# Six places of a decoder step re-ordered: casts, small operations and transposes

## The chip, the core and the metric

The kernel runs on one core of a Trainium2 chip. The core has five engines that run their own instruction streams in order: TensorE (PE in the profile; its weight loads are listed as PEld), VectorE (DVE), ScalarE (ACT), GpSimd (POOL) and SyncE (SP, which here only issues DMAs). They meet through semaphores. The metric is the device time of one execution in microseconds (us); lower is better. A line number such as L478 is a line of the kernel before.

## The reference, cut to what matters

One layer of a decoder: a normalisation with modulation, a large input projection, a gated short convolution beside a matrix memory with four heads (mLSTM), an output projection, a residual with layer norm, and then a feed-forward part with its own modulation, convolution, gate, down projection and layer norm. There are 256 prompt tokens and 8 x 4 sample tokens, 288 in all; the width is 2048, the feed-forward width 5632.

```python
mod = silu(c) @ w_ada + b_ada                   # six rows: shift, scale and gate, twice
u = layernorm(x) * (1 + sc1) + sh1
p = u @ w_in                                    # B, C, h, q, k, v, o and the gates
y = concat(conv_part(p), mlstm_part(p))
x = layernorm(ALPHA * x + (1 + g1) * (y @ w_out)) * ln1_g + ln1_b
u2 = layernorm(x) * (1 + sc2) + sh2
a, g = split(u2 @ w_up)
x = layernorm(ALPHA * x + (1 + g2) * ((silu(conv(a)) * g) @ w_down)) * ln2_g + ln2_b
```

All arithmetic is in float32.

## The kernel before, in words

**Layout.** Activations lie with 128 features on the partitions and the 288 tokens along the free dimension, so x, u, u2 and the like are 16 tiles ("chunks", index k) of 128 x 288. Weights stream from HBM: 309 items of 128 x 2048 (1 MB), each 16 blocks of 128 x 128, through a ring of seven `raw` buffers. The order of the items is laid down by `plan()`.

**A matmul in three passes.** Each weight half (8 blocks, 128 x 1024) is split into a rounded high part `whi` (ACT, L316) and a remainder `wlo` (DVE, L329), in rings of four buffers each. Activations are split in the same way (`uh`, `ul`; `u2h`, `u2l`; and so on). A block then costs three TensorE matmuls of 288 columns: high x low (L476), low x high (L477), high x high (L478). `next_block()` hands out the blocks. At the first block of a half it calls `split_to`, which splits the halves up to two ahead (`LOOK`; one ahead in the first 16 halves). At the fourth block (`PREHI`) it issues the next half's cast alone, so that ACT is ahead of DVE.

**Ticks.** Everything beside the weight stream is written as generators ("sides"). `next_block()` calls `tick()` once per block, before the block's three matmuls, and a side that has yielded n goes on n blocks later. The order in which a program line is emitted is the order in its engine's queue, so the numbers yielded decide what lies before what on every engine.

**The six places.**

1. *Sums of the first norm* (L1233 to L1248). In the output projection the 16 tiles `mix` are added to the residual (`residual`, L1107) and `stats(m)` gathers sums: squares on ACT (L1156, L1157), weighted sums on DVE (L1142, L1152). `barrier` (set at L1114) keeps `split_to` from going beyond the last weights of the projection. The cast at `PREHI` does not look at it. In the last tile, 11 blocks in, `late_sums` makes four TensorE sums (L1238); 12 blocks in, `up_split` lifts the barrier and splits one half of the up-projection.
2. *u2* (L1364 to L1385). Per chunk: `u2_t` (a 256-column product L1366 and two 32-column products for the sample tokens L1367, L1368, all DVE), a TensorE correction (L1373) into PSUM, its addition (L1377, DVE), the cast (L1379, ACT) and the remainder (L1385, DVE). Six tiles of the up-projection run chunk by chunk over it, 18 matmuls per chunk; one PSUM bank is left for the corrections.
3. *Restoring of x1* (`restore`, L1423). Three POOL operations per chunk (L1426 to L1428), one chunk each 12 blocks, the first 8 blocks after the side starts. It must be done when the first part's up-projection ends (`drain(back)`).
4. *Modulation's transposes* (`ada_finish`, L389). When a unit of the modulation is complete in PSUM, it is copied out (L398, DVE; the first by ACT, L400), transposed on TensorE (L406) `YA` = 5 blocks later, and added to its bias (L412, L416). Kind "h" are the five units for u, kind "f" the other four.
5. *Heads' turns* (L911 to L927). For each of four heads: two DVE operations `norm` (L897), 6 blocks later four TensorE transposes `hT` (L915) with four DVE operations that read them (L918, L919), 6 blocks later the next head. `drain(ml)` at the end of the first `o` tile forces what is left of it.
6. *u of group three*: the first projection runs over the chunks in groups (0-1, 2-3, 4-7, 8-11, 12-15), since a group's modulation arrives late. `make_u(k)` (L555) calls `modulate` (L487): one 256-column operation L488 and two 32-column ones L490 and L491, all DVE; then the cast L558 (ACT) and the remainder L563 (DVE). One chunk per block (`YU` = 1) while the tiles of the group before are still running. Those tiles rotate over three PSUM banks. Every other one is taken out by ACT (L965, with the addition on POOL, L966), the rest by DVE (L968).

Of the kernel before, what the change touches and what calls it, by code (L numbers as in the profile page):

```python
# [9 lines left out]
AF = mybir.ActivationFunctionType  # L10
ALU = mybir.AluOpType

P = 128
NP = 256
# [3 lines left out]
N = NP + NS  # L18
# [19 lines left out]
UP_AT = 12  # L38
SUMS2_AT = 10
ROWS_AT = 20  # L40
RES0 = 8
RES1 = 12
G2_EARLY = 6
MIX_LAST = 8
# [5 lines left out]
AT0 = 1.0  # L50
SMALL_AT = 8
YA = 5
YU = 1
U_POOL = ()
HP_POOL = 2
# [160 lines left out]
def body(tc, d, off, items, blocks):  # L216
    nc = tc.nc
    V, A, G, T = nc.vector, nc.scalar, nc.gpsimd, nc.tensor
    from contextlib import ExitStack
    ctx = ExitStack()  # L220
    with ctx:
# [12 lines left out]
        def nm(s):  # L234
            uid[0] += 1
            return f"{s}_{uid[0]}"

        def st(name, dt=F32):
            return slab.tile([P, N], dt, tag="t", name=nm(name))
# [7 lines left out]
        def smp(ap):  # L247
            return ap[:, NP:N].rearrange("p (b t) -> p b t", t=TS)

        def bc_t(ap):  # L250
            return ap.unsqueeze(2).to_broadcast([P, NB, TS])
# [3 lines left out]
        def sm(name):  # L255
            a, b = off[name]
            return small[:, a:b]
# [12 lines left out]
        raws, halves = {}, {}  # L270
# [3 lines left out]
        barrier = [len(items)]  # L274
        sides = []
        it_index = {}
        hlist = []
# [28 lines left out]
        def free():  # L306
            live[0] -= 1
            load()

        his = {}  # L310

        def split_hi(n):
            if n not in his:
                i, hf = hlist[n]
                his[n] = hip.tile([P, 1024], F32R, tag="w", name=nm("whi"))
                A.copy(his[n], raws[i][:, hf * 1024:(hf + 1) * 1024])  # L316
                return his[n]
            return his.pop(n)

        def split_to(n):  # L320

            while emitted[1] < min(n + 1, len(hlist)) and hlist[emitted[1]][0] < barrier[0]:
                i, hf = hlist[emitted[1]]
                if i not in raws:
                    return
                r = raws[i][:, hf * 1024:(hf + 1) * 1024]
                hi = split_hi(emitted[1])
                lo = lop.tile([P, 1024], F32R, tag="w", name=nm("wlo"))
                V.tensor_tensor(lo, r, hi.bitcast(F32), ALU.subtract)  # L329
                halves[emitted[1]] = (hi, lo)  # L330
                emitted[1] += 1
                if hf == 1:
                    raws.pop(i)
                    free()
# [28 lines left out]
        mod = pers.tile([P, 6, KB, 9], F32, name="mod")  # L363
# [25 lines left out]
        def ada_finish(unit):  # L389
            kind, first, nb = UNITS[unit]  # L390
            n = P * nb // 2 if kind == "h" else 512
            ps = ada_ps.pop(unit)
            t = []
            for i in range(0, n, 256):
                s = st("adat")
                w = min(256, n - i)
                if unit:
                    V.tensor_copy(s[:, 0:w], ps[:, i:i + w])  # L398
                else:
                    A.copy(s[:, 0:w], ps[:, i:i + w])  # L400
                t.append(s)
            yield YA
            nbs = n // P
            tp = mps("adatp")
            for b in range(nbs):
                T.transpose(tp[:, b * P:(b + 1) * P], t[b // 2][:, (b % 2) * P:(b % 2 + 1) * P], ident)  # L406
            for b in range(nbs):
                src = tp[:, b * P:(b + 1) * P].rearrange("p (s j) -> p s j", j=32)[:, :, 0:9]
                if kind == "h":
                    for ty in range(2):  # L410
                        sl = slice(first + b, first + b + nbs + 1, nbs)
                        V.tensor_tensor(mod[:, ty, sl, :], src[:, 2 * ty:2 * ty + 2, :],  # L412
                                        badd[:, ty, sl].unsqueeze(2).to_broadcast([P, 2, 9]), ALU.add)
                else:
                    sl = slice(b, 16, 4)
                    V.tensor_tensor(mod[:, first, sl, :], src,  # L416
                                    badd[:, first, sl].unsqueeze(2).to_broadcast([P, 4, 9]), ALU.add)
            if kind == "h":
                prev = None
                for k in range(first, first + nb):  # L420
                    if k == 1:
                        V.tensor_tensor(xh[1], xh[1], rstd0, ALU.mult)
                        make_ulo(*prev)
                        prev = None
                    uh = make_u(k)
                    if prev:
                        make_ulo(*prev)
                    prev = (k, uh)
                    yield YU
                make_ulo(*prev)  # L430
# [20 lines left out]
        def next_block():  # L451
            while items[pos[0]][0] != "w":
                take()
            i, b = pos
            n = first_half[i] + b // 8
            if b % 8 == 0:
                load()
                split_to(n + (LOOK if n >= EARLY else LOOK_EARLY))
            if b % 8 == PREHI and n >= EARLY:
                n3 = emitted[1]  # L460
                if n3 < len(hlist) and n3 not in his and hlist[n3][0] in raws:
                    split_hi(n3)
            hi, lo = halves[n]
            pos[1] += 1
            if b % 8 == 7:
                halves.pop(n)
            if b == 15:
                pos[0], pos[1] = i + 1, 0
            tick()
            b %= 8  # L470
            return hi[:, b * P:(b + 1) * P], lo[:, b * P:(b + 1) * P]
# [13 lines left out]
            return h, lo  # L485

        def modulate(dst, src, sc, sh, k, E=V):  # L487
            E.tensor_scalar(dst[:, 0:NP], src[:, 0:NP], mod[:, sc, k, 0:1], mod[:, sh, k, 0:1],  # L488
                            ALU.mult, ALU.add)
            E.tensor_tensor(smp(dst), smp(src), bc_t(mod[:, sc, k, 1:9]), ALU.mult)  # L490
            E.tensor_tensor(smp(dst), smp(dst), bc_t(mod[:, sh, k, 1:9]), ALU.add)  # L491

# [28 lines left out]
        for k in range(0, KB, 2):  # L521
            t = st("xsum")
# [366 lines left out]
        def mlstm_end():  # L889
            hS = normalise(S["num"], colS[:, 1:2], 8)  # L890
            yield 8
            V.tensor_scalar(mvt[:, :, 0], mv[:, :, 1], EPS, None, ALU.add)
            newton(mvt[:, :, 1], mvt[:, :, 0], mvt[:, :, 2])
            yield 8

            def norm(ht, i):
                V.tensor_scalar(ht[:, 0:256], ht[:, 0:256], mv[:, i, 0:1], mvt[:, i, 1:2],  # L897
                                ALU.subtract, ALU.mult)

            norm(hS, 8)  # L900
            yield 6
            pS = mps("hsT", 256)
            for et in range(2):
                T.transpose(pS[:, et * P:(et + 1) * P], hS[:, et * P:(et + 1) * P], ident)
            hsT = st("hsT")
            A.copy(hsT[:, 0:256], pS)
            mhn = sm("mhn")
            for h in range(H):
                for tt in range(2):
                    norm(hraw[h][tt], 2 * h + tt)  # L910
                yield 6  # L911
                for et in range(2):
                    ps = mps("hT", 256)
                    for tt in range(2):
                        T.transpose(ps[:, tt * P:(tt + 1) * P], hraw[h][tt][:, et * P:(et + 1) * P], ident)  # L915
                    i = 2 * h + et
                    o = st("hm")
                    V.tensor_scalar(o[:, 0:NP], ps, mhn[:, i:i + 1], None, ALU.mult)  # L918
                    V.tensor_scalar(o[:, NP:N], hsT[:, et * P + 32 * h:et * P + 32 * h + 32],  # L919
                                    mhn[:, i:i + 1], None, ALU.mult)  # L920
                    hm[i] = o
                yield 6
                hraw[h] = None
# [119 lines left out]
        for m in range(KB):  # L1043
            t = st("xa")
# [200 lines left out]
        def up_split():  # L1245
            yield UP_AT
            barrier[0] = len(items)
            split_to(upcoming_w())  # L1248

        def upcoming_w():  # L1250
            return emitted[1]
# [91 lines left out]
        R = st("R")  # L1343
# [12 lines left out]
        x1 = xa  # L1356
# [4 lines left out]
        fsv = fs[:, 0:KB * NB].rearrange("p (k b) -> p k b", b=NB)  # L1361
        V.tensor_tensor(fsv, mod[:, SC2, :, 1:9], g1v.unsqueeze(2).to_broadcast([P, KB, NB]), ALU.mult)

        def u2_t(k):  # L1364
            t = st("u2t")
            V.scalar_tensor_tensor(t[:, 0:NP], x1[k][:, 0:NP], gs[:, k:k + 1], R[:, 0:NP], ALU.mult, ALU.mult)  # L1366
            V.tensor_tensor(t[:, NP:N], x1[k][:, NP:N], R[:, NP:N], ALU.mult)  # L1367
            V.tensor_tensor(smp(t), smp(t), bc_t(fsv[:, k]), ALU.mult)  # L1368
            hold[k] = t

        def u2_corr(k):
# [41 lines left out]
        for j in (8, 12):  # L1413
            ps = mps("rb", N)
            tokens(ps, spread(j), P)
            t = st("rb")
# [6 lines left out]
        def restore():  # L1423
            yield RES0
            for k in range(KB):
# [414 lines left out]
```

## Time and profile before

| | |
|---|---|
| median of 3 runs | 1537.24 us (1536.14 to 1538.02) |
| the profiled execution | 1537.2 us |
| its span, first to last instruction | 1535.4 us |
| DVE busy | 946.3 us (62%) |
| ACT busy | 592.7 us (39%) |
| POOL busy | 226.4 us (15%) |
| DMA | 344.03 MB, mean 224 GB/s |
| mean granted TensorE clock | 0.997 |

The span is what the trace shows; 1.8 us of the execution's time lie around it. In a list of waits, "A <- B: t, n, m" says that A's engine sat idle before A for t us in n places, the longest m, until B released it. In a timeline a row has the start, the duration, engine, line, operation, the tiles written and read, the shape, a count, and in brackets the idle time before it and what ended it. In a table of windows each row has the stretch, its length, and for each engine the busy time and the number of instructions, then the granted TensorE clock as a share of full speed, the DMA share and GB/s.

### The profile page before, as it was taken

The page shows a single profiled execution, that of the slowest core. Times are in us where ns is not written, and L with a number is a line of the kernel's source. Part 1 is how long each engine was busy: PE and PEld are TensorE (multiplying, and loading weights), DVE is VectorE, ACT ScalarE, POOL GpSimd, SP SyncE. Part 2 cuts the span into 40 slices and gives each one's busy share as a digit, 9 for nine tenths or more (in the row PEclk, how much of TensorE's full clock was granted, in tenths as well). Part 3 has the DMA queues.
Part 4 walks back from the last instruction along what each step waited for, and adds up shares of the span by engine and source line. Part 5 has one row for each costly group of instructions (what it writes and reads, how often), then busy time and mean ns, then how long its engine had stood idle before and what let it go on. Part 6 is the DMA issues. An engine that isn't in the chain of part 4 may idle for free.

```text
span 1535.4 us, 28421 instructions
## 1 busy us (share of the span) xinstructions
PE 1516.2 (99%) x11849; PEld 1416.9 (92%) x11849; DVE 946.3 (62%) x1771; ACT 592.7 (39%) x891; POOL 226.4 (15%) x445
## 2 busy tenths in 40 slices
PE   9999999999999999999999999999999999999998
PEld 7988988888888889789999999999999999999997
DVE  6466567677775488697565545555555445555764
ACT  5542234422233434344334333444443334444442
POOL 3320005201025130005730000000000000000400
PEclk9999999999999999999999999999999999999999
DMA  9887778568899774474666544444445444444411
GB/s 392 340 343 287 304 292 338 222 254 298 330 375 357 291 276 170 163 274 183 228 221 229 190 163 169 161 165 165 165 172 181 154 166 167 166 168 166 156 58 62
DMA packets 50036, 344.03 MB, mean 224 GB/s; under 512 B 5950, under 2 KB 6254, under 8 KB 9454
## 3 DMA queue, kind: packets, MB, share of 16 engines
q1 hardware_dynamic: 47028, 329.21, 57.8%
q0 software_dynamic: 2736, 12.82, 2.1%
q8 instruction: 93, 1.52, 0.4%
q14 instruction: 35, 0.29, 0.1%
q10 hardware_dynamic: 144, 0.19, 0.0%
HBM read 329.88 MB, written 12.31 MB: 223 GB/s over the span
## 4 chain that ended last, share of the span: by engine, by line
PE 93%; DVE 4%; DMA 2%; ACT 1%; issue 1%; SPq 0%; DVEq 0%; ACTq 0%
PE dn L478 6%; PE dn L476 6%; PE dn L477 6%; PE g L476 6%; PE g L478 6%; PE g L477 6%; PE a L476 6%; PE a L478 5%; PE a L477 5%; PE adaps L383 5%; PE h L476 5%; PE h L477 4%; PE h L478 4%; PE mix L476 2%; PE mix L477 2%; PE mix L478 2%
## 5 line engine op out<-in xcount | busy, mean ns | idle before, releaser
L316 ACT CAST whi<-raw 128x1024 fp32r<-128x1024 f32 x410 | 424.0, 1046 | 373.9 <-PE dn L478 125.8
L329 DVE TENSOR_TENSOR wlo<-raw,whi 128x1024 fp32r<-128x1024 f32 x410 | 502.6, 1242 | 52.2 <-ACT whi L316 51.5
L478 PE MATMUL dn<-y2h,whi 128*128 128x288 f32 x704 | 207.9, 295 | 0.0
L476 PE MATMUL dn<-y2l,whi 128*128 128x288 f32 x704 | 207.7, 295 | 0.0
L477 PE MATMUL dn<-y2h,wlo 128*128 128x288 f32 x704 | 207.4, 295 | 0.0
L477 PE MATMUL a<-u2h,wlo 128*128 128x288 f32 x656 | 193.6, 295 | 0.8 <-DVE wlo L329 0.8
L478 PE MATMUL g<-u2h,whi 128*128 128x288 f32 x656 | 193.9, 296 | 0.0
L478 PE MATMUL a<-u2h,whi 128*128 128x288 f32 x656 | 193.8, 295 | 0.0
L476 PE MATMUL a<-u2l,whi 128*128 128x288 f32 x656 | 193.6, 295 | 0.0
L477 PE MATMUL g<-u2h,wlo 128*128 128x288 f32 x656 | 193.4, 295 | 0.0
L476 PE MATMUL g<-u2l,whi 128*128 128x288 f32 x656 | 193.3, 295 | 0.0
L476 PE MATMUL h<-ul,whi 128*128 128x288 f32 x512 | 156.4, 305 | 2.4 <-DVE hp L968 1.5
L477 PE MATMUL h<-uh,wlo 128*128 128x288 f32 x512 | 152.2, 297 | 0.0
L478 PE MATMUL h<-uh,whi 128*128 128x288 f32 x512 | 151.9, 297 | 0.0
L477 PEld LDWEIGHTS dn<-y2h,wlo 128*128 128x128 f32 x704 | 132.3, 188 | 0.1
L476 PEld LDWEIGHTS dn<-y2l,whi 128*128 128x128 f32 x704 | 132.3, 188 | 0.1
L478 PEld LDWEIGHTS dn<-y2h,whi 128*128 128x128 f32 x704 | 132.2, 188 | 0.0
L476 PEld LDWEIGHTS a<-u2l,whi 128*128 128x128 f32 x656 | 123.2, 188 | 5.0 <-issue 4.2
L476 PEld LDWEIGHTS g<-u2l,whi 128*128 128x128 f32 x656 | 123.2, 188 | 3.4 <-ACT hal L1545 2.5
L477 PEld LDWEIGHTS a<-u2h,wlo 128*128 128x128 f32 x656 | 123.0, 188 | 1.1 <-DVE wlo L329 1.1
L478 PEld LDWEIGHTS g<-u2h,whi 128*128 128x128 f32 x656 | 123.4, 188 | 0.0
L478 PEld LDWEIGHTS a<-u2h,whi 128*128 128x128 f32 x656 | 123.3, 188 | 0.0
(475 smaller groups left out, 2788.0 us busy)
## 6 DMA issues: line engine op xcount, KB each, us to landing
raw<-wst SPq DMA_DIRECT2D x300, 1024.0 KB, 4.8
raw<-cst SPq DMA_DIRECT2D x8, 1024.0 KB, 4.9
cs_o<-raw POOLq DMA_DIRECT2D x8, 1024.0 KB, 10.4
xa<-xT POOLq DMA_DIRECT2D x16, 144.0 KB, 9.9
y_o<-yo SPq DMA_DIRECT2D x9, 256.0 KB, 2.5
xin<-xT SPq DMA_DIRECT2D x5, 432.0 KB, 5.6
cp_o<-cnew POOLq DMA_DIRECT2D x8, 128.5 KB, 7.2
raw<-wst SPq DMA_DIRECT2D x2, 512.0 KB, 13.7
```

The source lines that it names most:

```text
L316: A.copy(his[n], raws[i][:, hf * 1024:(hf + 1) * 1024])
L329: V.tensor_tensor(lo, r, hi.bitcast(F32), ALU.subtract)
L383: T.matmul(ps[32 * s:32 * s + 32, 0:n], csil[:, k, :], r[:, c0:c0 + n], start=(k == 0), stop=(k == 15))
L476: T.matmul(ps, hi, ul, start=start, stop=False)
L477: T.matmul(ps, lo, uh, start=False, stop=False)
L478: T.matmul(ps, hi, uh, start=False, stop=stop)
```

## The change

Six edits, all of order or of engine; no value that is computed changes.

```diff
-RES0 = 8
+RES0 = 70
...
+YF = 12
+U_ACT = (4, 5, 6, 7)
...
-            yield YA
+            yield YA if kind == "h" else YF
...
-                if n3 < len(hlist) and n3 not in his and hlist[n3][0] in raws:
+                if n3 < len(hlist) and n3 not in his and hlist[n3][0] in raws and hlist[n3][0] < barrier[0]:
                     split_hi(n3)
...
         def modulate(dst, src, sc, sh, k, E=V):
-            E.tensor_scalar(dst[:, 0:NP], src[:, 0:NP], mod[:, sc, k, 0:1], mod[:, sh, k, 0:1],
-                            ALU.mult, ALU.add)
+            if k in U_ACT:
+                A.activation(dst[:, 0:NP], src[:, 0:NP], AF.Identity, scale=mod[:, sc, k, 0:1], bias=mod[:, sh, k, 0:1])
+            else:
+                E.tensor_scalar(dst[:, 0:NP], src[:, 0:NP], mod[:, sc, k, 0:1], mod[:, sh, k, 0:1],
+                                ALU.mult, ALU.add)
...
                 for tt in range(2):
                     norm(hraw[h][tt], 2 * h + tt)
-                yield 6
+                yield 9
...
         def up_split():
             yield UP_AT
             barrier[0] = len(items)
             split_to(upcoming_w())
+            yield 3
+            split_to(upcoming_w())
...
         def u2_t(k):
...
-            V.tensor_tensor(t[:, NP:N], x1[k][:, NP:N], R[:, NP:N], ALU.mult)
-            V.tensor_tensor(smp(t), smp(t), bc_t(fsv[:, k]), ALU.mult)
+            G.tensor_tensor(t[:, NP:N], x1[k][:, NP:N], R[:, NP:N], ALU.mult)
+            G.tensor_tensor(smp(t), smp(t), bc_t(fsv[:, k]), ALU.mult)
```

- Place 1: the cast at `PREHI` respects the barrier, and `up_split` splits a second half three blocks after the first.
- Place 2: the two 32-column products of u2 go from DVE to POOL.
- Place 3: the restoring starts 70 blocks after its side, not 8.
- Place 4: kind "f" units are transposed 12 blocks after they are copied out, not 5.
- Place 5: the heads' transposes follow their norm after 9 blocks, not 6.
- Place 6: for chunks 4 to 7 the 256-column operation of the modulation goes from DVE to ACT.

## The prediction

> **What bounds the kernel now.** I read the page first, then the list of waits with TensorE as the waiter, then windows and timelines at the six places.
>
> ```profile
> PE 1516.2 (99%) x11849; PEld 1416.9 (92%) x11849; DVE 946.3 (62%) x1771; ACT 592.7 (39%) x891; POOL 226.4 (15%) x445
> ...
> PE adatp L406 <- DVE adat L398: 1.7, 2, 1.0
> PE h L476 <- DVE hp L968: 1.5, 1, 1.5
> PE corr L1373 <- DVE u2t L1377: 1.2, 2, 1.0
> PE stat L1238 <- DVE ln1p L1152: 1.1, 1, 1.1
> ...
> PE a L477 <- DVE wlo L329: 0.8, 1, 0.8
> ...
> PE hT L915 <- DVE ht L897: 0.7, 1, 0.7
> ...
> PE h L476 <- ACT hpt L965: 0.4, 1, 0.4
> ```
>
> TensorE is busy 1516.2 of 1535.4 us. No edit touches a weight matmul, so only TensorE's idle time, 19 us, and the time in which its clock is low can be won. Seven rows of its waits belong to the six places: 1.7 + 1.5 + 1.2 + 1.1 + 0.8 + 0.7 + 0.4 = 7.4 us. The clock is in the windows; the first three are adjacent, 3.41 us each:
>
> ```profile
> 88.65:92.06 3.41, 1.83 (x12) 1.60 (x12) 2.61 (x8) 1.91 (x4) 0.81 (x1) 1.00 1.01 425
> 92.06:95.47 3.41, 3.41 (x16) 3.20 (x15) 3.41 (x5) 3.17 (x5) 3.07 (x4) 0.50 0.91 384
> 95.47:98.88 3.41, 3.41 (x27) 3.41 (x26) 2.97 (x5) 1.14 (x2) 0.00 (x0) 1.00 0.45 161
> 638.20:641.61 3.41, 2.29 (x12) 1.19 (x11) 2.02 (x3) 1.28 (x3) 0.00 (x0) 1.00 0.00 0
> ```
>
> After a stretch in which PE was busy for 1.83 of 3.41 us (54%), the granted clock was 0.50 for exactly the next 3.41 us: 16 matmuls instead of 27. Those 11 matmuls at 3.41 / 27 = 0.126 us are 1.4 us that no list of waits shows. The fourth row (67% busy) was not followed by a fall. So the limit lies somewhere between 54% and 67%.
>
> A wait also costs more than its row, because it breaks the pipeline. Here are the last matmul before the modulation's four transposes and the first after them, once with a wait and once without:
>
> ```profile
> 470.04 0.29 PE L478 MATMUL o<-uh,whi 128*128 128x288 f32 x1
> ...
> 471.49 0.38 PE L476 MATMUL o<-ul,whi 128*128 128x288 f32 x1
> ...
> 300.79 0.29 PE L478 MATMUL cg<-uh,whi 128*128 128x288 f32 x1
> ...
> 301.28 0.38 PE L476 MATMUL cg<-ul,whi 128*128 128x288 f32 x1
> ```
>
> From start to start it is 1.45 us against 0.49 us: 0.96 us lost where 0.6 us of idle time is listed. I add 0.3 us to each wait that goes, and 0.2 us where no transposes follow.
>
> **The change part by part.** *Place 4, modulation's transposes.* Two of the four late units wait, 0.6 and 1.0 us. The copies out sit behind other DVE work and end 0.3 us after TensorE would need them. Seven blocks more are 21 matmuls of 0.126 us, 2.6 us. That covers both waits, and the transposes still fall inside the same output tile. What moves along are four DVE additions per unit and one POOL DMA (the feed-forward state) that waits for the copy's buffer; it is needed 100 us later. The two units that do not wait move too and have no reason to begin. Gain: 1.7 + 2 x 0.3 = **2.3 us**.
>
> *Place 5, heads' turns.* The third head waits:
>
> ```profile
> 450.86 2.00 ACT L316 CAST whi<-raw 128x1024 fp32r<-128x1024 f32 x2 [7.44 <-DMA raw<-wst]
> ...
> 451.94 1.23 DVE L329 TENSOR_TENSOR wlo<-raw,whi 128x1024 fp32r<-128x1024 f32 x1 [0.36 <-ACT whi L316]
> 453.08 0.82 DVE L897 TENSOR_SCALAR ht<-ht,mv,mvt 128x256 f32<-128x256 f32 x2
> ...
> 469.16 0.46 DVE L1102 TENSOR_TENSOR sg<-sg,hm 128x288 f32<-128x288 f32 x1 [5.27 <-ACT sg L1101]
> ```
>
> A late weight DMA holds ACT, the remainder then holds DVE, and the norm is queued behind it. With 9 blocks the norm of this head itself comes 6 blocks later (two heads before it), behind the same remainder, and ends near 455. Its transposes come 15 blocks into their tile, near 457. The fourth head ends 12 blocks later than now, 14 blocks into the first `o` tile, two before `drain` would force it. Its DVE reads end near 468; the first `o` product that shares DVE is at 469.2. Sixteen transposes, eight norms and sixteen reads move, and no DMA. Gain: 0.7 + 0.3 = **1.0 us**.
>
> *Place 1, sums of the first norm.*
>
> ```profile
> 637.67 1.04 ACT L316 CAST whi<-raw 128x1024 fp32r<-128x1024 f32 x1 [7.88 <-DMA raw<-wst]
> ...
> 638.62 0.44 ACT L1156 ACTIVATE ln1q<-xa 128x288 f32<-128x288 f32 x1
> ...
> 640.03 0.65 PE L1238 MATMUL stat<-ln1p,pick 128*8 128x288 f32 x2 [1.12 <-DVE ln1p L1152]
> ```
>
> The early cast of the up-projection's first half holds ACT for 7.9 us until its weights land, and the squares of tile 14 are queued behind it. With the barrier respected, the squares run as soon as tile 14's residual is there, some 4 us sooner, and DVE's sums end well before TensorE is ready for the fourth one (640.03 - 1.12 = 638.9). The fourth sum then follows the third. The cast comes after the squares and still starts at 637.67, because the DMA sets it. Two casts and two remainders (1.04 and 1.22 us each) end near 641.2, before DVE's next duty, the residual of the last tile, which must wait for 0.65 us of sums and 18 matmuls, near 641.9. Cover: 0.7 us. If the weights land later than that, the excess is paid. The second half's split also frees its `raw` buffer, so SP issues one load some 18 us earlier. Gain: 1.1 + 0.2 = **1.3 us**.
>
> *Place 2, u2.* Two waits, 1.0 and 0.3 us:
>
> ```profile
> 658.20 2.36 DVE L329 TENSOR_TENSOR wlo<-raw,whi 128x1024 fp32r<-128x1024 f32 x2 [0.36 <-ACT whi L316]
> 660.48 0.45 DVE L1377 TENSOR_TENSOR u2t<-u2t,corr 128x288 f32<-128x288 f32 x1
> ...
> 660.98 0.40 PE L1373 MATMUL corr<-tok,cft 128*128 128x288 f32 x1 [0.97 <-DVE u2t L1377]
> ...
> 664.00:676.00 12.00, 11.98 (x90) 11.98 (x91) 11.43 (x32) 6.83 (x11) 0.00 (x0) 1.00 0.73 292
> ...
> L993 POOL COPY hal<-sffn x44: 188/281/1251, 591.4 to 1408.2; 128x16 f32<-128x16 f32 x44
> ...
> L602 POOL TENSOR_TENSOR cs<-xf x1: 215/215/215, 234.7 to 234.7; 4x24 f32<-4x24 f32 x1
> ```
>
> Two remainders stand before the addition L1377 that frees the correction's bank. One of them is the half that place 1 now splits in advance. The addition comes 1.2 us earlier, near 659.3, before TensorE is ready for the correction (660.98 - 0.97 = 660.0). The later wait hangs on the same chain (addition, cast, cast, remainder, addition), which moves 1.15 us while TensorE moves 1.2; I leave 0.1 to 0.2 us there. Gain: 1.2 + 2 x 0.2 - 0.3 = **1.3 us**, nearly all of it from the edit of place 1. The move to POOL itself I take at nothing. POOL sits idle here and DVE, busy 11.43 of 12.00 us, is not on TensorE's path (11.98 of 12.00). POOL's price is not in the trace: the nearest rows give 0.2 us for 24 columns and 1.25 us for the longest small copy beside DVE, so a pair costs 0.4 to 2.5 us per chunk. I take 0.5. A chunk lasts 2.5 us.
>
> *Place 3, restoring.*
>
> ```profile
> L999 DVE SCALAR_TENSOR_TENSOR ac<-hal,small,ac x44: 533/535/1122, 701.3 to 1421.2; 128x304 f32<-128x304 f32 x44
> ...
> 715.01 0.96 DVE L999 SCALAR_TENSOR_TENSOR ac<-hal,small,ac 128x304 f32<-128x304 f32 x1
> ...
> 716.89 1.21 DVE L329 TENSOR_TENSOR wlo<-raw,whi 128x1024 fp32r<-128x1024 f32 x1
> ```
>
> Beside POOL's products the convolution steps take 0.96 us instead of 0.535. Two of them stand directly before the remainder that TensorE awaits (0.8 us), and two pairs before those. Without POOL it comes at least 0.85 us sooner. The 48 operations start 62 blocks later, behind POOL's small copies of those tiles. They end at block 70 + 16 x 12 = 262 of the 384 that the part has left, and place 3 runs from there on as it now runs from 729, without a wait of TensorE. Gain: 0.8 + 0.2 = **1.0 us**.
>
> *Place 6, u of group three.*
>
> ```profile
> 86.07 0.42 DVE L412 TENSOR_TENSOR mod<-adatp,badd 128x18 f32<-128x18 f32 x4
> ...
> 88.25 0.40 ACT L965 ACTIVATE hpt<-h 128x288 f32<-128x288 f32 x1
> ...
> 90.59 0.43 ACT L558 CAST uh<-xc 128x288 fp32r<-128x288 f32 x1 [1.22 <-DVE xc L491]
> 90.78 0.45 DVE L968 SCALAR_TENSOR_TENSOR hp<-h,hp 128x288 f32<-128x288 f32 x1
> 90.92 1.04 ACT L316 CAST whi<-raw 128x1024 fp32r<-128x1024 f32 x1
> ...
> L781 ACT ACTIVATE d<-d,colP x4: 506/508/512, 304.3 to 385.9; 128x256 f32<-128x256 f32 x4
> ...
> 311.82 0.31 POOL L804 MEMSET vt<- 128x1 f32 x2 [2.91 <-PE kv L798]
> ...
> 313.10 0.37 ACT L803 COPY vt<-kv 128x256 f32<-128x256 f32 x1
> ```
>
> Four DVE operations become four on ACT; a 256-column one with an operand per partition takes 0.51 us there (L781). ACT then does 0.51 + 0.03 + 0.43 per chunk, and neighbours overlap by 0.1 (90.59 + 0.43 against 90.92), so 0.87 us. From 86.5 two chunks end at 88.26. The eviction hpt starts where it does now, and its 0.4 us wait stays. Chunk 6's cast ends near 89.55, its remainder at 90.05, and the eviction hp starts at 89.95 instead of 90.78: 0.8 us won. Behind it, ACT's next eviction (after the weight cast) ends at 91.65, where TensorE now wants it at 91.35: 0.3 us given back. Idle time in any 3.41 us is then at most about 1.2 us (65% busy), mostly under 1.0, so I take the fall of the clock as gone, 1.4 us. The last two rows carry the order: POOL's fill of one column of `vt`, emitted after the copy, ran before it, so disjoint columns of a tile do not wait for each other. Gain: 0.8 - 0.3 + 1.4 = **1.9 us**.
>
> The sum is 2.3 + 1.0 + 1.3 + 1.3 + 1.0 + 1.9 = 8.8 us. Made against the profiled execution, 1537.2 (span 1535.4 and 1.8 around it), which is also the median of the runs, it gives **1528.4 us**.
>
> **The rivals.** *The clock falls all the same.* Place 6 keeps some 1.1 us of waits; a window that catches most of them is 65% busy, close to the 54% that was followed by a fall. Time: 1528.4 + 1.4 = 1529.8. [...]
>
> *ACT and DVE take turns in place 6.* If the two column ranges of a chunk did wait for each other, a chunk would cost 0.51 + 0.4 + 0.43 us and more, as now. Nothing of the 1.9 is won: 1530.3. The `vt` rows speak against it.
>
> *POOL and DVE get in each other's way in u2.* DVE is 95% busy there; if POOL's pair lengthens DVE's steps by more than the 0.38 us it takes away, 13 chunks lose 0.1 to 0.3 us each: 1530 to 1532.5.
>
> *The waits come back a few blocks on* (norms and copies behind the next remainder, weights late at 641). Half of places 1, 4 and 5, and place 3, lost: 1532 to 1536.
>
> *Slower.* The mechanism is POOL's pair in u2. Above 2.5 us per pair, POOL sets the pace of the loop, and TensorE waits in each of 14 chunks. At 3.6 us (two of the 1.8 us that its longest 288-column product took) it costs 14 x 1.1 = 15.4 us: 1543.8. It decides from 3.3 us on (8.8 + 3.1 = 14 x 0.85). Against it: 32 columns, an idle engine, and 0.2 us for 24 columns.
>
> **How the numbers follow.** A measurement of this kernel can tell about 0.2% (3.1 us) from no change. Forecast, 1527 to 1529.4: 0.52. Clock: 0.16. Turns of ACT and DVE: 0.08. POOL against DVE: 0.10. Waits come back: 0.11, of which 0.07 within 0.2%. Slower: 0.03. The range 1526.8 to 1532.2 takes in the first four and what the added 0.2 to 0.3 us per wait may be off; it leaves out about 0.2. Faster 0.90, same 0.07, slower 0.03.
>
> **What would show it.** In the waits of TensorE, the rows of adatp on DVE, stat on ln1p, a on wlo and hT on ht are gone; corr on u2t keeps at most 0.3 us; hp keeps under 1 us; hpt keeps 0.4 and more. No window before the end has a clock under 1.00. ACT's cast after the projection starts with its DMA and after the squares. L999 is at 0.535 us until 728. POOL's two products per chunk take 0.2 to 0.6 us each. I am wrong if new rows of TensorE's waits add up to more than 1 us, or if the clock falls at another place.

## The result, and the profile after

The changed kernel took 1528.65 us (median of 6 runs, 1528.45 to 1529.39), the kernel before 1536.61 (6 runs, 1535.16 to 1538.02). The ratio is 0.9946, with a 95% interval of 0.9937 to 0.9956. So 8.0 us are gone in the medians; 8.8 were forecast, from 1537.2 to 1528.4 us. The profiled execution took 1528.45 us with a span of 1526.4.

Two rows of the changed kernel's page, the engines' busy time and the granted clock in 40 slices:

```profile
PE 1512.3 (99%) x11849; PEld 1414.9 (93%) x11849; DVE 944.6 (62%) x1735; ACT 594.5 (39%) x895; POOL 240.0 (16%) x477
...
PEclk9999999999999999999999999999999999999999
```

TensorE's busy time fell by 3.9 us though it runs the same 11849 products: the stretch at half the clock (3.41 us at 92.06 in the kernel before) and the refill behind each wait (0.17 to 0.5 us where it was read below) are counted there, and no list of waits shows them. The rest of the 9.0 us of span is idle time. The list of TensorE's waits in the changed kernel (engine and line, releaser: us in total, times, longest):

```profile
PE sq L542 <- ACT sq L540: 1.0, 1, 1.0
PE warm L524 <- POOL ones L369: 1.0, 1, 1.0
PE h L478 <- DVE hp L973: 0.8, 1, 0.8
PE h L478 <- ACT hpt L970: 0.8, 2, 0.6
PE rr L1343 <- DVE sv L1333: 0.7, 1, 0.7
...
PE corr L1380 <- DVE u2t L1384: 0.2, 1, 0.2
```

Of the seven rows of before, those of adatp on DVE, stat on ln1p, a on wlo and hT on ht are gone. corr on u2t went from 1.2 to 0.2, hp from 1.5 to 0.8, and hpt grew from 0.4 to 0.8 (0.55 and 0.23). This is the timeline of ACT and DVE at place 6, group three, in the changed kernel:

```profile
88.43 0.59 ACT L491 ACTIVATE xc<-xc,mod 128x256 f32<-128x256 f32 x1
...
89.05 0.43 ACT L563 CAST uh<-xc 128x288 fp32r<-128x288 f32 x1
...
89.39 0.60 ACT L491 ACTIVATE xc<-xc,mod 128x256 f32<-128x256 f32 x1
89.49 0.19 DVE L496 TENSOR_TENSOR xc<-xc,mod 128x32 f32<-128x32 f32 x1
...
89.97 0.45 DVE L973 SCALAR_TENSOR_TENSOR hp<-h,hp 128x288 f32<-128x288 f32 x1
...
91.30 0.70 ACT L970 ACTIVATE hpt<-h 128x288 f32<-128x288 f32 x2
```

ACT's 256 columns (89.39 to 89.99) and DVE's 32 of the same tile (89.49) run side by side, so the two ranges do not wait for each other. The eviction hp starts at 89.97, forecast 89.95. The next eviction hpt starts at 91.30 and holds TensorE for 0.23 us: this is the wait that was to be given back. The windows of the changed kernel there (us, length, busy PE, PEld, DVE, ACT, POOL with counts, granted clock, DMA share, GB/s):

```profile
86.67:90.09 3.42, 2.42 (x17) 1.96 (x15) 2.76 (x10) 3.29 (x9) 0.80 (x1) 1.00 1.01 405
90.09:93.50 3.41, 2.80 (x19) 2.57 (x20) 2.40 (x3) 3.41 (x6) 1.72 (x2) 1.00 1.02 430
93.50:96.91 3.41, 3.41 (x28) 3.41 (x27) 3.41 (x6) 2.18 (x3) 1.36 (x3) 1.00 0.55 185
```

71% and 82% busy, and the clock stays at 1.00.

### The profile page after: what moved, and what is told of

Same layout as the page of the kernel before. It is cut to its first block, busy times and chain, and to the rows that moved or that the text cites. A ratio compares the mean times of both kernels' runs of the same rounds, so it can differ in the third digit from the quotient of the medians.

```text
span 1526.4 us, 28419 instructions
## 1 busy us (share of the span) xinstructions
PE 1512.3 (99%) x11849; PEld 1414.9 (93%) x11849; DVE 944.6 (62%) x1735; ACT 594.5 (39%) x895; POOL 240.0 (16%) x477
## 3 DMA queue, kind: packets, MB, share of 16 engines
q8 instruction: 93, 1.52, 0.4%
## 4 chain that ended last, share of the span: by engine, by line
PE 96%; DVE 2%; ACT 1%; issue 0%; DMA 0%; SPq 0%; DVEq 0%; ACTq 0%
PE dn L480 6%; PE dn L479 6%; PE dn L478 6%; PE a L478 6%; PE a L480 6%; PE g L480 6%; PE g L478 6%; PE a L479 6%; PE g L479 6%; PE adaps L385 6%; PE h L478 5%; PE h L479 4%; PE h L480 4%; PE mix L478 2%; PE mix L479 2%; PE mix L480 2%
```

## The experiments

Twelve kernels ran, five rounds each. A median of five turned out too coarse for parts of 0.5 to 2 us, because two kinds of event land in some executions and not in others (a fall of the clock, 1.6 us; a late weight load, 1.3 us; both are shown below). So each part is read from the traces, by how much later than in the changed kernel the same product starts, counted in each trace from its own first `h` product (25.46 us in the changed kernel). The columns are the 445th `h` product (behind group three, 101.85), the first hsT (435.34), the first statc (640.09), the last corr (684.46) and the first yb (1509.00); the last column is where the profiled execution's clock fell before the end.

| kernel | h 445 | hsT | statc | last corr | yb | clock fell at |
|---|---|---|---|---|---|---|
| before | 1.68 | 1.70 | 6.05 | 7.07 | 8.71 | 92.06 |
| after_again | -0.02 | 0.28 | 0.25 | 0.27 | 0.26 | - |
| u6_group3 | 2.48 | 2.50 | 2.77 | 2.79 | 2.78 | 93.19 |
| u6_fill | 0.30 | 0.32 | 0.46 | 2.07 | 2.06 | 648.32 |
| yu2 | -0.13 | -0.26 | -0.22 | 1.40 | 1.93 | 647.61 |
| u4_turns | 0.01 | 0.03 | 2.29 | 2.29 | 2.14 | - |
| u5_heads | -0.08 | -0.06 | 0.39 | 0.46 | 0.80 | - |
| u1_cast | -0.03 | -0.02 | 1.43 | 1.44 | 0.75 | - |
| u1_second | 0.04 | 0.34 | 0.33 | 3.28 | 3.28 | 648.09 |
| u2_pool | -0.04 | -0.02 | 0.26 | 0.18 | 0.30 | - |
| u3_restore | -0.05 | -0.04 | 0.09 | 0.12 | 1.32 | - |
| tail_fill | 0.00 | 0.12 | 0.09 | 0.14 | 0.13 | - |
| best | 1.45 | 1.52 | 1.45 | 1.48 | 2.02 | - |

The second row is the changed kernel against itself: two of its executions differ by up to 0.3 us, so differences below that tell nothing. The yb column is less sure than the others: between the last corr and yb, u1_cast gains 0.7 us on the changed kernel and yu2 and best lose 0.5, in stretches where TensorE has no more waits than the changed kernel and where no edit of theirs acts. So a place is priced below close behind it, and not at yb.

Each execution also has a mean granted clock, traced or not. In every trace the clock is at half for the last 5.2 to 7.9 us (6.4 in the kernel before, 6.2 in the changed kernel), which takes 0.0017 to 0.0026 off the mean, and a fall before the end takes off another 0.0011. So, as an estimate from these traces, an execution with a mean of 0.998 had no fall, one with 0.997 at most one, and one with 0.995 at least two.

### Place 6 undone, and undone with its idle time filled

```
-U_ACT = (4, 5, 6, 7)
+U_ACT = ()
```

> The changed kernel with place 6 undone: chunks 4 to 7 are modulated on DVE again. Theory (two waits and the fall of the clock they bring): TensorE's waits on hpt and hp come back with 0.4 and 1.5 us, the 3.41 us after them run at clock 0.50, and the time rises by 1.9 us, to about 1530.5 us. [...]

The second kernel has the same edit and six products of the ones matrix with itself at the place of the long wait:

```
+FILL = 6
...
+                if g == 1 and t[1] == 22:
+                    fl = mps("fill", P)
+                    for _ in range(FILL):
+                        T.matmul(fl, ones, ones, start=True, stop=True)
```

> Place 6 undone as in u6_group3, and six further matmuls of 128 columns, whose result nothing reads, put on TensorE ahead of the tile that waits for hp (1.3 us of work inside a wait of 1.5 us). Theory (the clock falls when TensorE is busy for little more than half of a 3.41 us stretch): the tile starts when it did, the clock stays at 1.00, and the time is 1.4 us below that of u6_group3, about 1529.1 us. Rival (the fall comes from something else than idle time at this place): the clock falls all the same and the time is that of u6_group3, 1530.5 us.

Measured: 1530.22 us (ratio 0.9956, 0.9944 to 0.9969) and 1530.37 (0.9957, 0.9943 to 0.9970). The medians don't part them; the windows do. u6_group3:

```profile
89.78:93.19 3.41, 1.89 (x13) 1.44 (x12) 2.61 (x7) 2.08 (x5) 0.59 (x2) 1.00 1.01 425
93.19:96.60 3.41, 3.41 (x16) 3.41 (x15) 3.41 (x6) 2.99 (x4) 2.78 (x4) 0.50 0.82 344
```

u6_fill, at 90 and at 648 us:

```profile
88.54:91.95 3.41, 3.10 (x23) 2.92 (x24) 2.58 (x8) 1.91 (x5) 0.80 (x1) 1.00 1.02 430
91.95:95.36 3.41, 3.41 (x26) 3.20 (x25) 3.40 (x5) 3.30 (x5) 3.05 (x4) 1.00 0.72 296
644.91:648.32 3.41, 2.15 (x17) 1.61 (x13) 2.24 (x10) 1.19 (x4) 0.91 (x4) 1.00 1.01 411
648.32:651.73 3.41, 3.41 (x17) 0.59 (x16) 1.38 (x3) 1.37 (x2) 2.94 (x13) 0.50 1.02 430
```

Without place 6 the stretch at 90 us is 55% busy and the next runs at half the clock, with 16 products. With the hole filled it is 91% busy, the next keeps 1.00 with 26, and group three costs 0.30 us more than in the changed kernel, where the kernel before costs 1.68. So of place 6's 1.7 us, 0.3 are waits and 1.4 the clock. (u6_group3's 2.48 also has a wait of 0.45 us at 80 us that the kernel before does not have.) u6_fill lost 1.6 us later, between the start of rr (0.47) and the last corr (2.07): the last two rows show the clock at half there, at a place that no edit touched. No forecast had it for this kernel. Two of its untraced executions (1530.14 and 1530.76 us) have a mean clock of 0.998, so no fall, and what made them as long as the traced one is open.

### Group three's chunks two turns apart

```
-YU = 1
+YU = 2
```

> The changed kernel with YU = 2: one chunk of u per two blocks instead of per block, in all groups. Theory (what is left of place 6's waits, 0.55 + 0.83 + 0.23 us, is ACT and DVE doing four chunks within four blocks of TensorE): spread over eight blocks these waits go, with about 0.15 us of refill each, and the time falls by 1.5 to 2.0 us, to about 1526.9 us. Rival (the chunks then end too late for the group that needs them, here or in groups four and five): new waits of TensorE on ul or uh at the start of a group, time 1528.7 us or more.

Measured: 1530.44 us (0.9961, 0.9948 to 0.9973). The wait and the windows of yu2:

```profile
PE h L478 <- ACT hpt L970: 2.3, 1, 2.3
```

```profile
87.83:91.24 3.41, 1.53 (x12) 1.30 (x10) 1.99 (x6) 2.24 (x5) 0.35 (x1) 1.00 1.00 418
91.24:94.65 3.41, 2.98 (x22) 2.99 (x23) 2.57 (x7) 3.38 (x7) 2.19 (x4) 1.00 0.84 351
...
644.20:647.61 3.41, 2.15 (x21) 1.77 (x21) 2.04 (x11) 1.33 (x3) 1.10 (x4) 1.00 0.93 368
647.61:651.03 3.42, 3.42 (x17) 0.58 (x9) 1.30 (x3) 1.18 (x2) 3.03 (x12) 0.50 1.01 417
```

The three waits of group three became one, 2.3 us long against 1.6 in sum, and group three still ended no later (-0.13 us). Of that, 0.26 us had been won before 84 us, where a wait of 0.26 us near 54 us is gone; that the rest went with two waits' refills is likely and not shown. The 1.5 us that this was to win are not there. The stretch was 45% busy, less than in the kernel before, and no fall followed; a stretch at 644 us was 63% busy and a fall did follow. So the busy share by itself does not decide. The slowest execution of yu2 (1533.21 us, untraced) has a mean clock of 0.995, so at least two falls, and where they came is not known.

### Place 4 undone

```
-YF = 12
+YF = 5
```

> The changed kernel with place 4 alone undone: the modulation's transposes are given five turns again in place of twelve. Theory: TensorE's waits of 0.63 us near 470 us and 1.03 us near 587 us come back, and with the refill behind each the start of statc near 640 us is 2.3 us later than in the changed kernel's trace; 1530.9 us, or 1532.5 with a fall of the clock. Rival 1 (a wait costs its row and no more): 1.7 us later, 1530.3. Rival 2 (a wait removed there comes back at a later barrier, so place 4 was worth nothing): 0.0 to 0.5 us later, 1528.65 to 1529.1.

Measured: 1530.71 us (0.9959, 0.9946 to 0.9973). A row of u4_turns' list of waits, and a row of its timeline:

```profile
PE adatp L408 <- DVE adat L400: 1.7, 2, 1.1
```

```profile
642.59 0.38 PE L1297 MATMUL statc<-small,rows 8*128 8x8 f32 x2 [0.48 <-ACT rows L1294]
```

In the changed kernel the same product is at

```profile
640.09 0.83 PE L1297 MATMUL statc<-small,rows 8*128 8x8 f32 x6 [0.48 <-ACT rows L1294]
```

Counted from each trace's first `h`, and with the 0.03 us by which hsT was already later, that is 2.26 us for two waits of 0.69 and 1.05: each cost 0.26 us beyond its row. Both rivals (1.7, and at most 0.5) fall.

### Place 5 undone

```
-                yield 9
+                yield 6
```

> The changed kernel with place 5 alone undone: the heads' turns are six blocks apart again in place of nine. Theory: TensorE's wait of 0.67 us at hT on ht near 454 us comes back, and the start of statc near 640 us is 1.0 us later than in the changed kernel's trace; 1529.6 us, or 1531.2 with a fall of the clock near 648. Rival (the norm of the third head waits for the same late weights either way, and what place 5 saved is lost at the heads that now stand later): 0.0 to 0.3 us later, 1528.65 to 1528.95.

Measured: 1530.50 us (0.9956, 0.9943 to 0.9968). A row of its waits:

```profile
PE hT L920 <- DVE ht L902: 0.2, 1, 0.2
```

Only 0.2 of the 0.67 us came back, and statc is 0.45 us later (0.39 + 0.06), between theory and rival. In the kernel before the third head's norm stood behind a remainder that a late weight load had held; in this execution the cast ahead of it waited 5.10 us for its weights and not 7.44. Read just behind the heads' last transposes, at the `o` product that runs at 465 us in the changed kernel, u5_heads is 0.63 us later than at hsT, and the kernel before 1.17; some 0.2 us of the 0.63 is made up again before statc. The median says more (1.4 us above 1529.13 of after_again), but the profiled execution took 1529.12, the fastest of its five. The other four have no trace; three of them (1530.24 to 1531.18) have a mean clock of 0.998, so it was no fall that made them longer.

### Place 1 undone in two parts

The barrier's condition in the early cast:

```
-                if n3 < len(hlist) and n3 not in his and hlist[n3][0] in raws and hlist[n3][0] < barrier[0]:
+                if n3 < len(hlist) and n3 not in his and hlist[n3][0] in raws:
```

> The changed kernel with one part of place 1 alone undone: the early cast of the up-projection's first half may again be issued ahead of the barrier, so before the squares of tile 14; the second split stays. Theory: TensorE's wait of 1.1 us at stat on ln1p near 640 us comes back, statc starts 1.3 us later than in the changed kernel's trace, and the stretch from statc to the last corr does not change; 1529.9 us, or 1531.5 with a fall of the clock near 648. Rival (the barrier only moves the cast behind the sums, and its remainder then holds the last residual): 0.0 to 0.5 us later, 1528.65 to 1529.15.

The second split of the group that follows:

```
-            yield 3
-            split_to(upcoming_w())
```

> The changed kernel without the second split before the first norm's end (up_split splits one half, as before); the barrier for the early cast stays, and so does POOL's part of u2. Theory (the half split in advance is what frees the correction's bank in time): two remainders stand before the addition again, TensorE waits about 1 us for it, +1.2 us, about 1529.9 us. Rival (DVE got free because two products per chunk went to POOL): the wait stays away, within 0.3 us of 1528.65 us.

Measured: u1_cast 1529.42 us (0.9950, 0.9938 to 0.9962), u1_second 1530.19 (0.9960, 0.9948 to 0.9973). Two waits of u1_cast, and ACT's timeline ahead of the first:

```profile
PE stat L1243 <- DVE ln1p L1157: 1.0, 1, 1.0
...
PE gbm L1090 <- DVE gbt L1087: 0.2, 1, 0.2
```

```profile
632.81 1.04 ACT L318 CAST whi<-raw 128x1024 fp32r<-128x1024 f32 x1 [7.84 <-DMA raw<-wst]
633.76 0.44 ACT L1161 ACTIVATE ln1q<-xa 128x288 f32<-128x288 f32 x1
```

The squares (L1161) stand behind a cast that waited 7.84 us for its weights. The same place in the changed kernel's timeline:

```profile
629.28 0.45 ACT L1161 ACTIVATE ln1q<-xa 128x288 f32<-128x288 f32 x1 [4.61 <-DVE xa L1117]
...
632.58 1.99 ACT L318 CAST whi<-raw 128x1024 fp32r<-128x1024 f32 x2 [2.43 <-DMA raw<-wst]
...
633.66 2.36 DVE L331 TENSOR_TENSOR wlo<-raw,whi 128x1024 fp32r<-128x1024 f32 x2 [1.89 <-ACT whi L318]
...
637.04 0.48 DVE L1113 SCALAR_TENSOR_TENSOR xa<-mix,mod,xa 128x256 f32<-128x256 f32 x1 [1.02 <-PE mix L480]
```

The squares are at 629.28, and the cast waits for its weights behind them. Its remainders end at 636.0, and DVE then sits idle for 1.02 us before the last residual. Without the condition statc is 1.45 us later. But 0.24 of that was lost before place 1, up to the first of the sums (632.25 us in the changed kernel): it appears at the wait for gbt, near 476 us, which u2_pool and u6_group3 have too and which this edit does not touch. From the first sum to statc it is 1.21 us; theory 1.3. By yb only 0.75 is left: the two long stretches of down-projection, 95.46 and 95.26 us in the changed kernel, took 95.31 and 94.84 here, with TensorE busy throughout. Why the same 720 products run 0.15 and 0.4 us faster was not found.

u1_second has its waits back, as a row of its list shows:

```profile
PE corr L1378 <- DVE u2t L1382: 1.3, 2, 1.0
```

It loses 2.95 us from statc to the last corr. 1.6 of it is the clock, as in u6_fill and yu2, which leaves 1.35; theory 1.3. Executions without a trace agree: two of 1529.84 and 1529.89 us, near the forecast's 1529.9, have a mean clock of 0.998, so no fall; the traced one (1531.68) and one of 1532.17 have 0.996. The windows of u1_second:

```profile
644.67:648.09 3.42, 2.16 (x21) 1.75 (x21) 2.17 (x10) 1.30 (x3) 1.07 (x5) 1.00 1.01 424
648.09:651.50 3.41, 3.41 (x17) 0.51 (x11) 1.34 (x3) 1.21 (x2) 2.94 (x12) 0.50 1.02 430
```

Beside them those of u5_heads, whose clock did not fall, in the same piece of the program:

```profile
644.46:647.88 3.42, 2.16 (x21) 1.50 (x13) 2.34 (x12) 1.16 (x5) 0.75 (x3) 1.00 0.96 400
647.88:651.29 3.41, 3.41 (x26) 1.82 (x27) 2.17 (x5) 1.93 (x3) 2.94 (x13) 1.00 1.01 425
```

The same 2.16 us busy, in windows that lie 0.4 us apart against the program, and one is followed by 0.50 and the other by 1.00.

### Place 2's products back on VectorE

```
-            G.tensor_tensor(t[:, NP:N], x1[k][:, NP:N], R[:, NP:N], ALU.mult)
-            G.tensor_tensor(smp(t), smp(t), bc_t(fsv[:, k]), ALU.mult)
+            V.tensor_tensor(t[:, NP:N], x1[k][:, NP:N], R[:, NP:N], ALU.mult)
+            V.tensor_tensor(smp(t), smp(t), bc_t(fsv[:, k]), ALU.mult)
```

> The changed kernel with one part of place 2 alone undone: both products on the 32 sample columns of u2 stand on VectorE again and not on GpSimd; the second split of the group that follows stays as in the changed kernel. Theory (the move was priced at nothing, since GpSimd's pair and VectorE's pair both fit beside TensorE): starts near 692 us at most 0.3 us later, 1528.65 to 1528.95. Rival (VectorE is what the corr chunks wait for between 647 and 692 us): the two products of some 0.15 us each come back as waits at corr, 1 us or more later, 1529.7 or longer.

Measured: 1530.24 us (0.9952, 0.9939 to 0.9964), with the profiled execution at 1529.06. From statc to the last corr it is 0.08 us shorter than the changed kernel (0.18 - 0.26). The groups by line (count | busy us, mean ns of one | idle us before it), first in the changed kernel, then in u2_pool:

```profile
L1374 POOL TENSOR_TENSOR u2t<-xa,R 128x32 f32<-128x32 f32 x16 | 6.4, 402 | 59.4 <-ACT R L1351 59.4
L1375 POOL TENSOR_TENSOR u2t<-u2t,fs 128x32 f32<-128x32 f32 x16 | 5.4, 337 | 1.3
```

```profile
L1375 DVE TENSOR_TENSOR u2t<-u2t,fs 128x32 f32<-128x32 f32 x16 | 3.1, 192 | 0.6
...
L1374 DVE TENSOR_TENSOR u2t<-xa,R 128x32 f32<-128x32 f32 x16 | 3.0, 185 | 0.0
```

GpSimd's pair takes 0.74 us per chunk and VectorE's 0.38, and TensorE waits for neither: its one wait at corr on u2t is 0.25 us in both. By the traces the move is worth nothing here. The median alone would fit the rival (1529.7 or longer); three untraced executions (1530.24 to 1531.03) make it so, and what made them longer is open.

### Place 3 undone

```
-RES0 = 70
+RES0 = 8
```

> The changed kernel with place 3 alone undone: the restoring of x1 starts after 8 blocks again in place of 70. From the traces of before and after the stretch between rb near 698 us and yb near 1518 us lost 1.66 us in all. Theory (all of it is place 3): TensorE's wait for wlo of some 0.8 us near 715 us comes back, and yb starts 1.0 to 1.7 us later relative to rb; 1529.7 to 1530.4 us, or 1.6 more with a fall of the clock near 648. Rival (the wait for wlo goes with the moved restoring, but part of the 1.66 us comes from elsewhere): 0.8 us or less, 1529.4 at most.

Measured: 1530.28 us (0.9957, 0.9943 to 0.9971). Its wait and its DVE timeline:

```profile
PE a L479 <- DVE wlo L331: 0.8, 1, 0.8
```

```profile
707.82 0.96 DVE L1004 SCALAR_TENSOR_TENSOR ac<-hal,small,ac 128x304 f32<-128x304 f32 x1
708.82 0.97 DVE L1005 SCALAR_TENSOR_TENSOR ac<-hal,small,ac 128x304 f32<-128x304 f32 x1
709.71 1.21 DVE L331 TENSOR_TENSOR wlo<-raw,whi 128x1024 fp32r<-128x1024 f32 x1
```

The two convolution steps at 0.96 us ahead of the awaited remainder are back, and yb is 1.20 us later (1.32 - 0.12). All of it is there at the product that runs at 715 us in the changed kernel. At the same product the kernel before is 8.21 us later, 1.14 more than at the last corr. The other 0.5 of its 1.64 us builds up from there to yb, 0.44 of it behind 858 us, when the restoring is long done and no wait is listed that the changed kernel lacks. That is the drift told of above, and not place 3.

### The changed kernel again, and its later waits filled

The first is the changed kernel without an edit:

> The changed kernel itself once more, beside the same runs of the kernel before as the other three of this group. Theory A (the places alone): 1528.65 us, as before. Theory B (the granted clock is judged on a fixed grid of 3.41 us whose place against the program differs from execution to execution): the executions fall into two groups, about 1528.5 us without a fall of the clock and about 1530.1 us with one near 643 to 650 us, and the profiled one shows which it was. Theory C (this chip is slower than the one before by some 1.5 us): all executions near 1530.2 us with no fall in the profile.

The second:

```
         rps = mps("rr", N)
+        for _ in range(3):
+            T.matmul(rps[:, 0:P], ones, ones, start=True, stop=True)
...
             cps[k] = mps("corr", N)
+            for _ in range(2 if k == 0 else 0):
+                T.matmul(cps[k][:, 0:P], ones, ones, start=True, stop=True)
```

> The changed kernel, with three products of the ones matrix with itself (128 columns, about 0.21 us each) put into TensorE's wait ahead of the transposed rows rr and two into its wait ahead of the first corr; their results are overwritten by the work that follows. Theory B (the clock falls when a window of the 3.41 us grid is too idle): no fall between 640 and 655 us wherever the grid lies, 1528.5 us and no execution above 1529.5. Rival: the clock does not hang on these waits; it falls there as in the changed kernel, or the five products make rr and corr late and the time is 0.3 to 0.8 us longer, 1528.9 to 1530.9.

Measured: after_again 1529.13 us (0.9954, 0.9942 to 0.9967), its five executions 1528.72, 1528.88, 1529.13, 1532.33 and 1532.40; tail_fill 1528.64 (0.9944, 0.9932 to 0.9957), all five from 1528.40 to 1529.25. That is how theory B put the second run, but of the first it had two groups 1.6 us apart, and these are 3.4 apart, with no trace of a late one. The mean clock of the two late ones is 0.997, so at most one fall of 1.6 us, and at least 1.8 of their 3.4 us have another cause. Theory C (a slower chip) falls: in the three groups of runs, each on a chip of its own, the kernel before took 1537.16 (this group), 1536.54 and 1536.96 us, beside 1536.61 in the first measurement. The filling cost at most 0.14 us; whether it saved a fall is open, since the six executions of the changed kernel in the first measurement had none above 1529.39 either.

### A version to beat both

yu2 and tail_fill together, with nine products of ones in the one wait of group three (edit as in u6_fill, at `t[1] == 23`).

> The changed kernel with group three's chunks two turns apart (YU 2), nine products of the ones matrix with itself in the one wait of 2.3 us that this leaves there, and the same filling of the waits ahead of rr and the first corr as in the run named tail_fill. Theory (with two turns each chunk has one wait less, worth 0.2 us, and filled windows keep the clock): no fall anywhere before the end, and no execution above 1529.5; 1528.4 us, beside 1528.6 of tail_fill. Rival (the nine products make the product behind them late, or the clock falls at 92 us all the same): 1529.0 to 1530.3.

Measured: 1528.96 us (0.9948, 0.9936 to 0.9961), five executions from 1528.39 to 1530.19. The profiled one, the slowest, had lost 1.5 us before the wait that the nine products fill. ACT's timeline of it at 80 us, then that of the changed kernel:

```profile
79.69 1.04 ACT L319 CAST whi<-raw 128x1024 fp32r<-128x1024 f32 x1 [2.64 <-DMA raw<-wst]
80.64 0.70 ACT L975 ACTIVATE hpt<-h 128x288 f32<-128x288 f32 x2
```

```profile
77.56 1.05 ACT L318 CAST whi<-raw 128x1024 fp32r<-128x1024 f32 x1 [0.16 <-DMA raw<-wst]
...
78.58 0.41 ACT L970 ACTIVATE hpt<-h 128x288 f32<-128x288 f32 x1
```

A weight load landed 2.1 us later in this execution, the cast waited for it, and the eviction hpt queued behind the cast held TensorE for 1.32 us. In yu2, whose chunks have the same turns, there is no wait at 80 us. In the traced execution of best the clock fell nowhere before the end. It does not beat the changed kernel by anything that was measured.

## Why the prediction was right, and where it was not

| part | predicted | before to after, traces | part undone alone |
|---|---|---|---|
| place 6 | 1.9 | 1.68 | 1.4 clock + 0.3 waits |
| place 5 (hsT to 465 us) | 1.0 | 1.17 | 0.63; 0.45 by statc |
| place 4 (465 us to the first sum) | 2.3 | 1.89 | 2.26 |
| place 1 (first sum to statc) | 1.3 | 1.29 | 1.21 |
| place 2 (place 1's split) | 1.3 | 1.02 | 1.35; products moved: -0.08 |
| place 3 (last corr to 715 us) | 1.0 | 1.14 | 1.20 |
| 715 us to yb (drift) | - | 0.50 | - |
| sum | 8.8 | 8.7 | |

*What bounds.* Right in the main: the six places won idle time and clock, 8.2 of the 8.7 us by which yb starts earlier. The other 0.5 us is drift that no term of the forecast has, so that the sums come out as close as 8.8 and 8.7 is in part luck.

*A wait costs more than its row.* Right: 0.26 us more for each adatp wait (forecast 0.3), 0.17 in place 1 (1.04 us of wait, 1.21 lost; forecast 0.2), but 0.38 in place 3 (0.82 and 1.20; forecast 0.2) and 0.4 to 0.5 at the heads (0.22 and 0.63, before 0.67 and 1.17; forecast 0.3).

*Place 4.* Right in place and, undone alone, in size: 2.26 us for 2.3. Between the traces of before and after it is 1.89.

*Place 5.* The mechanism holds; the size is that of one execution. The term rested on one wait, and that wait hangs on when one weight load lands: 0.67 us in the kernel before, which lost 1.17 us there (forecast 1.0), and 0.22 with the turns undone, which lost 0.63.

*Place 1.* Right, and the risk named there was not met: the cover behind the two remainders was 1.0 us and not 0.7.

*Place 2.* Right that place 1's split carries it, that one wait stays (0.25 us) and that the products are worth nothing on either engine. GpSimd's pair was mis-sized: 0.74 us on average for 0.5, though no chunk came late. The slower rival (GpSimd sets the pace above 2.5 us a pair) had no ground, and "GpSimd and VectorE get in each other's way" fell with it.

*Place 3.* Right in kind: the wait for wlo goes and comes back with the edit, 1.20 us for 1.0. The restoring starts at 713.8 us in the changed kernel, so steps of 0.535 us end there (the next one, at 714.05, took 0.96); they were to last some 7 us longer by the program's own time.

*Place 6.* The sum is right (1.68 for 1.9) and the split nearly so: waits 0.3 for 0.5, clock 1.4 as forecast. ACT's 256 columns take 0.60 us and not 0.51, and a chunk 0.96 us (88.43 to 89.39) and not 0.87; hp did not suffer, since the chunk ahead began early enough for the cast to end at 89.48, forecast 89.55. The stay of hpt's wait (0.55) and the return of 0.23 us were forecast. That ACT and DVE take turns is refuted by the timeline, and that the waits come back later by both traces of the changed kernel.

*The clock.* The effect was forecast rightly and its rule wrongly. The step that failed reads "So the limit lies somewhere between 54% and 67%". The fall itself was real: filling the idle time at 90 us kept the clock at 1.00, with the 3.41 us windows lying within 0.1 us where they lay in the kernel before (its window's edge is 0.77 us behind the end of the long wait, 0.70 in u6_fill). Nor did it fall at 92 us in any of the eleven traces that keep place 6's edit, though in six of them the window there was 60 to 62% busy, less than the 65% of the forecast. But no limit on the busy share fits all traces: falls followed 54%, 55% and three times 63%, and none followed 45% (yu2), 60 to 62% (these six, and best at 78 us) or, in u5_heads at 644 us, 63%. At the later place the start of rr lay 0.81, 0.84 and 1.00 us behind the edge of a window where a fall followed, and 0.24, 0.60, 1.24, 1.99 to 2.18, 3.13 and 3.38 us behind it where none did (tail_fill and best, whose waits there were filled, are left out). So in these traces the fall goes with how the grid lies against the program. No run moved the grid alone, so this is argued and not shown. Whether busy time is the right measure is open too, since the products around rr are small; that was not tried. The longest gap ahead of the falls at 648 us was 0.74 us. That there is a grid is read from the traces: whole numbers of steps of 3.41 us, 25, 26 and three times 188, lie between the start of the clock's record and the five falls (in the kernel before from 6.73 to 92.06 us).

The forecast also said that a fall at another place would prove it wrong. In three variants one came near 648 us. The change did not bring the waits there: the kernel before has the same two (0.74 us at rr, 0.48 at the first corr). The changed kernel kept them, so by the account above some of its executions should be 1.6 us longer. None is known to be: its two traces have no fall there, and five of its first six executions have a mean clock of 0.998. Its two executions of 1532.3 and 1532.4 stay unexplained.

## What to carry to other kernels

When an engine is 99% busy, as TensorE is here, what is left lies in single waits of about a microsecond (0.3 to 1.5 us at the six places): price each as its row plus 0.2 to 0.5 us of refill, find what is queued ahead of its releaser, and move that. Weigh such edits by the start of the same instruction in two traces, close behind the place that was edited and with the kernel against itself as the measure of noise; medians of five here lay up to 1.5 us from the traced execution of the same kernel. Moving u2's two products to an idle engine was worth nothing, because the wait on VectorE hung on other work of that engine, the second remainder.

## What the runs showed of the hardware

In these traces the granted clock changed in steps of 3.41 us, on a grid that starts at another point in each execution. In the kernel before its record starts at 6.73 us, with 25 steps at full clock, one at half (92.06 to 95.47) and 420 at full; in the changed kernel it starts at 4.75, with 444 at full. Each of the five falls before the end lasts one step. A fall cost 1.4 to 1.6 us; three followed a stretch whose longest idle gap was 0.74 us, while one of 2.3 us (yu2), cut by a window's edge at 91.24, went without. Six products of ones in the wait at 90 us kept the clock at 1.00 (u6_fill, 26 products in the next 3.41 us beside 16 in the kernel before), the one pair of traces whose windows lie alike. On ScalarE, 256 columns with an operand per partition for scale and one for bias took 0.597 us, where the prediction's nearest row had 0.508. The same 720 products of a down-projection took 95.26 and 95.46 us in the changed kernel and 94.84 and 95.31 in u1_cast, with no wait listed.
